# Context feed-forward of a hybrid trunk: half weights in the latents' norm tiles, one norm step to a pair of features, and the decays' chain called from the middle of the loop

## The chip, the cores and the metric

One core of one Trainium2 chip. The metric is the device time of one execution in microseconds (us), as the median of several runs. The engines are named as in the profile: PE (TensorE matmuls), DVE (VectorE), ACT (ScalarE), POOL (GpSimd) and SP (SyncE, which here only issues transfers).

## The reference

One layer (DEPTH is 1) of a diffusion backbone over 1024 latent tokens and 256 context tokens, width 1024, feed-forward width 2816, all in float32. Cut to what the change touches:

```python
x = x + 0.5 * m_l[2] * swiglu(modulate(rms_norm(x, norm1_w), m_l[0], m_l[1]), w1, w3, w2)
ctx = ctx + 0.5 * m_c[2] * swiglu(modulate(rms_norm(ctx, norm1_w), m_c[0], m_c[1]), w1, w3, w2)
y_l, _ = token_mixing(modulate(rms_norm(x, norm2_w), m_l[3], m_l[4]),     # latents
                      modulate(rms_norm(ctx, norm2_w), m_c[3], m_c[4]), ...)
x = x + m_l[5] * y_l
x = x + 0.5 * m_l[8] * swiglu(modulate(rms_norm(x, norm3_w), m_l[6], m_l[7]), v1, v3, v2)
return rms_norm(x, final_norm_w)

def swiglu(h, w1, w3, w2):
    return (silu(h @ w1) * (h @ w3)) @ w2
# in token_mixing, for the retention heads:
lg_f, lg_b = log_sigmoid(ret_decay_f), log_sigmoid(ret_decay_b)
```

## The kernel before

**Arithmetic.** A float32 matrix product is made of three products of a faster type: each operand is split into a hi part (a copy to fp32r, ACT, line 60) and a lo part (the rest, line 61, on DVE or, where `eng` says so, on POOL), and `mm3` (lines 65 to 67) adds hi·hi, lo·hi and hi·lo in PSUM. A tile pair `hh`/`hl` holds the two parts of an activation, `whi`/`wlo` those of a streamed weight; `raw` is the weight as it comes from memory. There are six `raw` buffers and six pairs of `whi`/`wlo`.

**Stages.** `run` goes through the opening of the latents' first feed-forward (0 to some 120 us), its body (to some 650 us), the context's feed-forward (some 645 to 845 us), the latents' last part and the context's projections, the token mixing from about 930 us on, and the second feed-forward. Activations lie transposed: features on the 128 partitions, tokens along a row. `x[0]` and `x[1]` are the two halves of the latents with eight tiles of 128 x 512 each (`KD` is 8), `x[2]` the context with eight tiles of 128 x 256.

**The context's feed-forward.** A feature `f` is 128 of the 2816 hidden columns; the loop takes them in eleven pairs, numbered 0 to 10 below. `classic` (a pair) loads four weights (w1 and w3 of two features), each as two halves of 128 x 512, so eight half weights. Half weight `2 * (i % 4) + j` is split into slot `h00` to `h07` of the pool `hp`, from the second feature on (`halves_slots`, line 274); its lo part is made on POOL (`CENG`). A slot can be written only when PE has read what the pair before left there. One weight gives one `psa` product of 24 matmuls. In the middle of the pair `Y` adds the pair before to the context: eight units of six matmuls each into `psb`, of which there are four banks, each added to `x` by DVE (line 600). `Y` streams its own weights through `raw`, `whi` (ACT) and `wlo` (DVE).

**The norm beside it.** After each pair one entry of `pend` is called: `norm2(1, i)`, the steps of the second norm of the latents' second half: squares, the column of reciprocal roots (`nr`, with a `pow` on POOL), its rows (`ndiag` on DVE, `nrb` on ACT), and for each of eight tiles `norm_k`: `nt` (DVE, line 217, two buffers), `hh` (ACT, line 218), `hl` (DVE, line 223). All eight pairs of tiles `h[1]` are allocated ahead of the loop by `alloc_h((1,), self.hp)`.

**The order.** Most of the program's order is made by a scheduler: each instruction goes into its engine's queue by its priority and by what it depends on, and the queue runs in that order. So the place of a call in the code is not the place of its instructions. The opening's order on PE, DVE and ACT is fixed by hand.

**The decays.** `lg_setup` (line 840) loads eight numbers, spread over 128 partitions, and computes their log-sigmoid by a `pow` on POOL and a series on DVE, all on tiles of 128 x 8; then four small tables `kd` and the factor `cdec` by an exponential on ACT. `mix_setup` calls it at the start of the mixing.

Of the kernel before, what the change touches and what calls it, by code (L numbers as in the profile page):

```python
# [19 lines left out]
KD = D // P  # L20
# [11 lines left out]
class Trunk:  # L32
# [241 lines left out]
    def halves_slots(self, i):  # L274
        if i < 2:
            return None, None
        return tuple(self.hslot(f"0{2 * (i % 4) + j}") for j in range(2))

    def load_halves(self, src, dst=(None, None), eng=None):
        return [self.load_half(src[:, 512 * i:512 * i + 512], dst[i], eng) for i in range(2)]  # L280
# [212 lines left out]
    def back6(self, keep=True):  # L493
        A = self.bank4(self.psA)
        self.prod(1, A, True)
        c1 = self.keep4(A)
        B = self.bank4(self.psB)
        self.prod(2, B, True)
        self.add4(0, 0, self.plus4(c1, B))
        self.prod(6, A, False)  # L500
        u2 = self.keep4(A)
        B = self.bank4(self.psB)
        self.prod(5, B, True)
        c5 = self.keep4(B)
        self.prod(7, A, False)
        if keep:
            u3 = self.keep4(A)
            self.add4(1, 1, self.plus4(c5, u3))
        else:
            self.add4(1, 1, self.plus4(c5, A))  # L510
            self.add4(0, 1, A)
        self.prod(3, B, False)
        self.add4(1, 0, self.plus4(u2, B))
        return A
# [322 lines left out]
            act(a, a, AF.Exp, scale=-1.0)  # L837
            act(a, a, AF.Ln, bias=1.0)

    def lg_setup(self):  # L840
        nc, I, cp = self.nc, self.I, self.cp2
        x = self.tile(cp, [P, 8], F32, "lgx")
        nc.sync.dma_start(x, I["decay"].broadcast_to([P, 8]))
        e = self.tile(cp, [P, 8], F32, "lge")
        nc.vector.memset(e, float(np.e))
        u = self.tile(cp, [P, 8], F32, "lgu")
        nc.vector.tensor_scalar(out=u, in0=x, scalar1=-1.0, scalar2=None, op0=ALU.mult)
        nc.vector.tensor_tensor(out=u, in0=u, in1=x, op=ALU.min)
        nc.gpsimd.tensor_tensor(out=u, in0=e, in1=u, op=ALU.pow)
        t = self.tile(cp, [P, 8], F32, "lgt")  # L850
        nc.vector.tensor_scalar(out=t, in0=u, scalar1=2.0, scalar2=None, op0=ALU.add)
        nc.vector.reciprocal(t, t)
        nc.vector.tensor_tensor(out=u, in0=u, in1=t, op=ALU.mult)
        nc.vector.tensor_tensor(out=t, in0=u, in1=u, op=ALU.mult)
        nc.vector.tensor_scalar(out=e, in0=t, scalar1=1.0 / 19, scalar2=1.0 / 17, op0=ALU.mult, op1=ALU.add)
        for m in (15, 13, 11, 9, 7, 5, 3, 1):
            nc.vector.tensor_tensor(out=e, in0=e, in1=t, op=ALU.mult)
            nc.vector.tensor_scalar(out=e, in0=e, scalar1=1.0 / m, scalar2=None, op0=ALU.add)
        nc.vector.tensor_tensor(out=e, in0=e, in1=u, op=ALU.mult)
        nc.vector.tensor_scalar(out=x, in0=x, scalar1=0.0, scalar2=None, op0=ALU.min)  # L860
        nc.vector.scalar_tensor_tensor(out=x, in0=e, scalar=-2.0, in1=x, op0=ALU.mult, op1=ALU.add)
        self.lg = x
        self.kd = {}
        for i, (nm, s, pos) in enumerate((("f", 0, 2), ("f0", 0, 3), ("b", 4, 0), ("b1", 4, 1))):
            t = self.tile(cp, [P, 4], F32, "kd" + nm)
            nc.vector.tensor_scalar(out=t, in0=x[:, s:s + 4], scalar1=self.tab[:, POSC + pos:POSC + pos + 1],
                                    scalar2=None, op0=ALU.mult)
            nc.scalar.activation(t, t, AF.Exp)
            self.kd[nm] = t
        self.cdec = self.tile(cp, [P, 8], F32, "cdec")  # L870
        nc.scalar.activation(self.cdec, x, AF.Exp, scale=float(P))
# [572 lines left out]
    def run(self):  # L1444
        nc, tc, I = self.nc, self.tc, self.I
# [70 lines left out]
        def norm_step(tg, i, a, b):  # L1516
            with self.low(NLOW if tg == 1 and i in (1, 2) else None):
                norm_part(tg, i, a, b)
# [16 lines left out]
        norm2 = lambda tg, i: norm_step(tg, i, self.mcol(4, int(tg == 2)), self.mcol(3, int(tg == 2)))  # L1535
# [31 lines left out]
        def spill(tg):  # L1567
            o = TGS[tg][0]
            for k in range(KD):
                nc.sync.dma_start(self.xd[k * P:(k + 1) * P, o:o + 512], self.x[tg][k])  # L1570

        self.alloc_h((1,), self.hp)
        norm2(1, 0)
        pend = [lambda i=i: norm2(1, i) for i in range(1, 3 + KD)] + [lambda: spill(1)]
        for f in range(0, NF, 2):
            self.classic(f, (2,), mid2=(lambda: self.Y(f - 2, CT)) if f else None, eng=[nc.gpsimd if e else None for e in CENG])
            pend.pop(0)()
        A = self.bank4(self.psA)
        self.prod(4, A, True)
        self.add4(0, 1, A)  # L1580
# [184 lines left out]
```

## Time and profile before

| What | Value |
|---|---|
| median of 3 runs | 2179.47 us (2178.03 to 2180.61) |
| the profiled execution | 2180.54 us, span 2178.8 us, mean granted clock of PE 0.99 |
| PE busy | 2121.3 us, 97% of the span |
| DVE busy | 1525.0 us, 70% |
| ACT busy | 980.7 us, 45% |
| POOL busy | 280.4 us, 13% |
| traffic | 373 MB, 171 GB/s mean |

All spans of instructions and waits below are of the one profiled execution. A row of the timeline reads: start in us, duration in us, engine, line, operation, output <- inputs, and in brackets the idle time of the engine ahead of it and what ended it. In a row by stretches (`A:B`) follow the length, the busy time of PE, PEld (weight loads into PE), DVE, ACT and POOL with the number of instructions, then the granted clock of PE (1.00 is full), the share of DMA and GB/s.

### The profile page before, as it was taken

How to read it: one execution, taken by the hardware profiler on the slowest of the kernel's cores; microseconds unless marked ns; L12 is line 12 of the kernel's file. 1: busy time of each engine (PE TensorE's matmuls, PEld its weight loads, DVE VectorE, ACT ScalarE, POOL GpSimd, SP SyncE). 2: the span in 40 equal slices, each digit the busy share in tenths (PEclk: the TensorE clock that was granted, in tenths of full speed). 3: DMA queues.
4: the chain of work that ended last, by engine and by line, in shares of the span. 5: the costliest groups of instructions: out<-in, count | busy, mean ns of one | idle time of the engine just before them, and what ended most of it. 6: DMA issues, size and time to landing. Idle time of an engine off the chain costs nothing. (4 is left out here: it accounts for less than half of the span.)

```text
span 2178.8 us, 32819 instructions
## 1 busy us (share of the span) xinstructions
PE 2121.3 (97%) x11558; PEld 1811.5 (83%) x11558; DVE 1525.0 (70%) x2735; ACT 980.7 (45%) x1811; POOL 280.4 (13%) x285
## 2 busy tenths in 40 slices
PE   8999999999999999999989999999999999999998
PEld 7888888888889999987778988788878888888888
DVE  7889999756766756834665546758777666675676
ACT  4433334345545444546454335425343433444553
POOL 0000000000026562611132113200000000010000
PEclk8999999999999999999999999999999999999999
DMA  9267768469966565553322312324134444467674
GB/s 331 83 231 239 267 221 268 167 221 325 306 210 193 156 183 171 180 152 100 92 65 63 98 57 88 122 83 162 63 120 161 146 160 159 150 217 251 207 241 147
DMA packets 202933, 373.39 MB, mean 171 GB/s; under 512 B 24016, under 2 KB 37264, under 8 KB 202768
## 3 DMA queue, kind: packets, MB, share of 16 engines
q1 hardware_dynamic: 202336, 371.16, 52.7%
q8 instruction: 90, 1.47, 0.3%
q14 instruction: 75, 0.61, 0.1%
q10 hardware_dynamic: 432, 0.13, 0.0%
HBM read 296.72 MB, written 66.09 MB: 167 GB/s over the span
## 5 line engine op out<-in xcount | busy, mean ns | idle before, releaser
L60 ACT ACTIVATE whi<-raw 128x512 fp32r<-128x512 f32 (+1 forms) x563 | 347.1, 622 | 621.1 <-PE psa L66 169.1
L61 DVE TENSOR_TENSOR wlo<-raw,whi 128x512 fp32r<-128x512 f32 (+1 forms) x533 | 368.1, 694 | 314.3 <-ACT whi L60 310.9
L65 PE MATMUL psa<-hh,whi 128*128 128x512 f32 (+1 forms) x1108 | 435.2, 393 | 0.1
L66 PE MATMUL psa<-hl,whi 128*128 128x512 f32 (+1 forms) x1108 | 434.6, 392 | 0.0
L67 PE MATMUL psa<-hh,wlo 128*128 128x512 f32 (+1 forms) x1108 | 434.3, 392 | 0.0
L65 PE MATMUL psb<-hh,whi 128*128 128x512 f32 (+1 forms) x680 | 260.0, 382 | 0.5 <-ACT whi L60 0.5
L67 PE MATMUL psb<-hh,wlo 128*128 128x512 f32 (+1 forms) x680 | 259.7, 382 | 0.6 <-DVE wlo L61 0.6
L66 PE MATMUL psb<-hl,whi 128*128 128x512 f32 (+1 forms) x680 | 259.7, 382 | 0.0
L65 PEld LDWEIGHTS psa<-hh,whi 128*128 128x128 f32 x1108 | 209.1, 189 | 42.1 <-ACT s L341 0.6
L67 PEld LDWEIGHTS psa<-hh,wlo 128*128 128x128 f32 x1108 | 209.0, 189 | 41.7
L66 PEld LDWEIGHTS psa<-hl,whi 128*128 128x128 f32 x1108 | 209.1, 189 | 41.3
L65 PEld LDWEIGHTS psb<-hh,whi 128*128 128x128 f32 x680 | 127.9, 188 | 25.9 <-ACT whi L60 1.0
L67 PEld LDWEIGHTS psb<-hh,wlo 128*128 128x128 f32 x680 | 127.8, 188 | 25.7 <-DVE wlo L61 1.0
L66 PEld LDWEIGHTS psb<-hl,whi 128*128 128x128 f32 x680 | 127.9, 188 | 24.8
L60 ACT ACTIVATE hh<-raw 128x512 fp32r<-128x512 f32 x180 | 110.4, 623 | 72.7 <-PE psa L66 44.3
L61 POOL TENSOR_TENSOR hl<-raw,hh 128x512 fp32r<-128x512 f32 x84 | 116.2, 1393 | 70.5 <-ACT hh L60 64.4
L1095 POOL TENSOR_TENSOR nr<-nr,mhalf 128x4 f32<-128x4 f32 (+1 forms) x11 | 10.6, 964 | 869.3 <-DVE nr L1094 869.3
L65 PE MATMUL psa<-hh,hh 128*128 128x256 f32 x376 | 107.8, 287 | 0.0
L67 PE MATMUL psa<-hh,hl 128*128 128x256 f32 x376 | 107.8, 287 | 0.0
L66 PE MATMUL psa<-hl,hh 128*128 128x256 f32 x376 | 107.8, 287 | 0.0
L66 PE MATMUL psa<-wlo,hh 128*128 128x256 f32 (+1 forms) x320 | 93.8, 293 | 1.6 <-DVE wlo L61 1.5
L65 PE MATMUL psa<-whi,hh 128*128 128x256 f32 (+1 forms) x320 | 93.5, 292 | 1.2 <-ACT s L1049 1.2
(402 smaller groups left out, 4251.7 us busy)
## 6 DMA issues: line engine op xcount, KB each, us to landing
raw<-in_w SPq DMA_DIRECT2D x374, 256.0 KB, 3.2
gd<-s SPq DMA_DIRECT2D x154, 256.0 KB, 2.8
ada<-in_adaT SPq DMA_DIRECT2D x76, 512.0 KB, 4.8
raw<-gd SPq DMA_DIRECT2D x91, 256.0 KB, 3.0
s<-in_w SPq DMA_DIRECT2D x66, 256.0 KB, 5.0
sd<-s SPq DMA_DIRECT2D x44, 256.0 KB, 2.9
raw<-sd SPq DMA_DIRECT2D x44, 256.0 KB, 3.1
hh<-in_w SPq DMA_DIRECT2D x44, 256.0 KB, 3.9
```

Source lines behind the costliest of these rows:

```text
L60: nc.scalar.activation(hi, src, AF.Copy)
L61: (eng or nc.vector).tensor_tensor(out=lo, in0=src, in1=hi.bitcast(F32), op=ALU.subtract)
L65: mm(ps, wa[0], xa[0], start=start, stop=False, skip_group_check=more)
L66: mm(ps, wa[0], xa[1], start=False, stop=False, skip_group_check=more)
L67: mm(ps, wa[1], xa[0], start=False, stop=stop, skip_group_check=more)
L1095: nc.gpsimd.tensor_tensor(out=r, in0=r, in1=self.mhalf[:, :n], op=ALU.pow)
```

## The change

Three edits. The last half weight (`i % 4 == 3`, `j == 1`) of the pairs 2 to 9 goes to slot `1{p-2}`, that is to the tiles that will hold `h[1][p-2]`, where it went to slot `07`. The tiles of `h[1]` are no longer allocated ahead of the loop: after pair 2 + k, `norm1(k)` takes slot `1{k}` for `h[1][k]` and calls that tile's norm. And `lg_setup` is cut in two: the load and the chain become `lg_start`, called in the loop at `f == 8` with its tiles in the pool `cp`; the tables `kd` and `cdec` stay in `lg_setup`.

```diff
@@ -274,7 +274,8 @@
     def halves_slots(self, i):
         if i < 2:
             return None, None
-        return tuple(self.hslot(f"0{2 * (i % 4) + j}") for j in range(2))
+        p, last = i // 4, i % 4 == 3
+        return tuple(self.hslot(f"1{p - 2}" if last and j and 2 <= p < 10 else f"0{2 * (i % 4) + j}") for j in range(2))
@@ -837,8 +838,8 @@
-    def lg_setup(self):
-        nc, I, cp = self.nc, self.I, self.cp2
+    def lg_start(self):
+        nc, I, cp = self.nc, self.I, self.cp
         x = self.tile(cp, [P, 8], F32, "lgx")
         nc.sync.dma_start(x, I["decay"].broadcast_to([P, 8]))
...
@@ -860,6 +861,9 @@
         self.lg = x
+
+    def lg_setup(self):
+        nc, cp, x = self.nc, self.cp2, self.lg
         self.kd = {}
@@ -1569,12 +1573,19 @@
-        self.alloc_h((1,), self.hp)
+        self.h[1] = []
         norm2(1, 0)
-        pend = [lambda i=i: norm2(1, i) for i in range(1, 3 + KD)] + [lambda: spill(1)]
+
+        def norm1(k):
+            self.h[1].append(self.hslot(f"1{k}"))
+            norm2(1, 3 + k)
+
+        pend = [lambda i=i: norm2(1, i) for i in (1, 2)] + [lambda k=k: norm1(k) for k in range(KD)] + [lambda: spill(1)]
         for f in range(0, NF, 2):
             self.classic(f, (2,), mid2=(lambda: self.Y(f - 2, CT)) if f else None, eng=[nc.gpsimd if e else None for e in CENG])
             pend.pop(0)()
+            if f == 8:
+                self.lg_start()
```

On PE no instruction changes its place. Three places on other engines follow; lines from 278 on are numbered one higher in the changed kernel, from 866 on four higher.

**DVE in the opening** (some 57 to 64 us). Before, the last tile's `x` is followed by the sum of two weights into `ada` and by the tile's `hl`:

```order
L217 SCALAR_TENSOR_TENSOR x_17_106<-x_17_106,modl_88,nrb_272 128x512
L714 TENSOR_TENSOR ada_139_573<-raw_578,ada_138_572 128x512
L714 TENSOR_TENSOR ada_139_573<-raw_582,ada_138_572 128x512
L223 SCALAR_TENSOR_TENSOR hl_33_133<-x_17_106,modl_88,hh_32_132 128x512
L178 TENSOR_TENSOR nacc_515<-nacc_515,nsq_605 128x512
```

In the changed kernel:

```order
L217 SCALAR_TENSOR_TENSOR x_17_106<-x_17_106,modl_88,nrb_272 128x512
L848 TENSOR_SCALAR lgu_7193<-lgx_7189 128x8
L849 TENSOR_TENSOR lgu_7193<-lgu_7193,lgx_7189 128x8
L861 TENSOR_SCALAR lgx_7189<-lgx_7189 128x8
L852 TENSOR_SCALAR lgt_7197<-lgu_7193 128x8
L853 RECIPROCAL lgt_7197<-lgt_7197 128x8
L854 TENSOR_TENSOR lgu_7193<-lgu_7193,lgt_7197 128x8
L855 TENSOR_TENSOR lgt_7197<-lgu_7193 128x8
L856 TENSOR_SCALAR lge_7191<-lgt_7197 128x8
L715 TENSOR_TENSOR ada_139_573<-raw_578,ada_138_572 128x512
L715 TENSOR_TENSOR ada_139_573<-raw_582,ada_138_572 128x512
L223 SCALAR_TENSOR_TENSOR hl_33_133<-x_17_106,modl_88,hh_32_132 128x512
```

Eight steps of the chain have moved in, of which the fourth (`lgt` at line 852) waits for POOL's `pow`; the rest of the chain follows between the later instructions of the opening. On POOL the `pow` stands between two `nr` of the opening, on SP the load stands behind the first weights' loads.

**ACT in pair 2** (some 675 to 685 us). Here the names carry their slot: `hh06` and `hh07` are the last weight's two halves, `whi` the weights of `Y`. Before:

```order
L581 ACTIVATE s_1422_6378<-psa_1421_6353 128x256
L60 ACTIVATE hh06_1483_6645<-raw_1487_6649 128x512
L60 ACTIVATE whi_1466_6564<-raw_1465_6562 128x512
L60 ACTIVATE whi_1469_6570<-raw_1468_6568 128x512
L60 ACTIVATE hh07_1485_6647<-raw_1488_6653 128x512
L60 ACTIVATE ghi_1430_6418<-s_1422_6378 128x256
```

In the changed kernel:

```order
L582 ACTIVATE s_1406_6362<-psa_1405_6337 128x256
L60 ACTIVATE hh10_1469_6631<-raw_1472_6637 128x512
L60 ACTIVATE hh06_1467_6629<-raw_1471_6633 128x512
L60 ACTIVATE whi_1450_6548<-raw_1449_6546 128x512
L60 ACTIVATE whi_1453_6554<-raw_1452_6552 128x512
L60 ACTIVATE whi_1497_6760<-raw_1496_6758 128x512
L60 ACTIVATE ghi_1414_6402<-s_1406_6362 128x256
```

The last half, now in slot `10`, has moved from behind the two weights of `Y` to ahead of them and of its own first half.

**DVE in pair 3** (some 703 to 715 us). `nt` and `hl` are the norm, `x_946` the addition that frees the first bank of `Y`. Before:

```order
L217 SCALAR_TENSOR_TENSOR nt_6687<-x_832_4111,modl_88,nrb_6435 128x512
L61 TENSOR_TENSOR glo_6684<-s_6643,ghi_6683 128x256
L61 TENSOR_TENSOR wlo_7029<-raw_7026,whi_7028 128x512
L217 SCALAR_TENSOR_TENSOR nt_6941<-x_833_4112,modl_88,nrb_6435 128x512
L223 SCALAR_TENSOR_TENSOR hl_1323_5975<-nt_6687,modl_88,hh_1322_5974 128x512
L217 SCALAR_TENSOR_TENSOR nt_7195<-x_834_4113,modl_88,nrb_6435 128x512
L61 TENSOR_TENSOR wlo_7035<-raw_7032,whi_7034 128x512
L223 SCALAR_TENSOR_TENSOR hl_1325_5977<-nt_6941,modl_88,hh_1324_5976 128x512
L587 TENSOR_TENSOR s_6728<-psa_6742,s_6728 128x256
L223 SCALAR_TENSOR_TENSOR hl_1327_5979<-nt_7195,modl_88,hh_1326_5978 128x512
L61 TENSOR_TENSOR glo_6769<-s_6728,ghi_6768 128x256
L600 SCALAR_TENSOR_TENSOR x_946_4498<-psb_6784,modc_89,x_946_4498 128x256
```

In the changed kernel:

```order
L61 TENSOR_TENSOR wlo_7017<-raw_7014,whi_7016 128x512
L217 SCALAR_TENSOR_TENSOR nt_6673<-x_832_4111,modl_88,nrb_6419 128x512
L61 TENSOR_TENSOR glo_6668<-s_6627,ghi_6667 128x256
L61 TENSOR_TENSOR wlo_7023<-raw_7020,whi_7022 128x512
L217 SCALAR_TENSOR_TENSOR nt_6929<-x_833_4112,modl_88,nrb_6419 128x512
L223 SCALAR_TENSOR_TENSOR hl_1477_6672<-nt_6673,modl_88,hh_1476_6671 128x512
L217 SCALAR_TENSOR_TENSOR nt_7185<-x_834_4113,modl_88,nrb_6419 128x512
L588 TENSOR_TENSOR s_6714<-psa_6728,s_6714 128x256
L601 SCALAR_TENSOR_TENSOR x_946_4498<-psb_6770,modc_89,x_946_4498 128x256
```

Two of the three `hl` and one `glo` have left the place ahead of `x_946`. In each of the later pairs there stands one `hl` and one `nt`, where the pair after this one held the rest of the eight before and the others held none.

## The prediction

> **What bounds the kernel now.** I read the page first: how busy each engine is, then the chain that ended last.
>
> ```profile
> PE 2121.3 (97%) x11558; PEld 1811.5 (83%) x11558; DVE 1525.0 (70%) x2735; ACT 980.7 (45%) x1811; POOL 280.4 (13%) x285
> ```
>
> TensorE works 97% of the span, so a change that leaves the matmuls alone can only move PE's gaps: the profiled execution took 2180.54 us (span 2178.8), of which 57.5 us are not matmul time. The next view is what PE waits for around the edit (waits of PE, 620 to 900 us: engine, line, releaser: us in total, times, longest).
>
> ```profile
> PE psb L65 <- DVE x L600: 7.3, 4, 3.7
> ```
>
> All of it is one kind of wait: the units of `Y` use four PSUM banks in turn, and a fifth unit starts only when DVE has added the first to `x` (line 600). The timeline of PE has the three large ones, and one of the opening (start, duration, what; in brackets the gap before it and who ended it); the fourth of `Y` is what is left of the 7.3, 0.7 us.
>
> ```profile
> 57.23 0.50 PE L66 MATMUL psa<-hl,wh 128*128 128x512 f32 x1 [1.58 <-DVE hl L223]
> 679.17 0.39 PE L65 MATMUL psb<-ghi,whi 128*128 128x256 f32 x1 [1.88 <-DVE x L600]
> 715.15 0.58 PE L65 MATMUL psb<-ghi,whi 128*128 128x256 f32 x1 [3.67 <-DVE x L600]
> 736.15 0.39 PE L65 MATMUL psb<-ghi,whi 128*128 128x256 f32 x1 [0.99 <-DVE x L600]
> ```
>
> A gap costs more than its length. Busy time by stretches, with the granted clock after POOL's column:
>
> ```profile
> 57.50:60.00 2.50, 2.50 (x12) 2.04 (x12) 1.18 (x3) 2.12 (x4) 0.00 (x0) 1.00 0.66 213
> 677.50:680.00 2.50, 0.83 (x6) 0.83 (x7) 2.04 (x3) 0.95 (x2) 2.36 (x2) 0.97 0.59 173
> 680.00:682.50 2.50, 2.50 (x14) 2.50 (x13) 1.74 (x5) 0.00 (x0) 0.24 (x1) 0.50 0.68 211
> 715.00:717.50 2.50, 2.35 (x11) 2.35 (x12) 2.33 (x6) 0.72 (x1) 0.00 (x0) 0.50 0.26 93
> 717.50:720.00 2.50, 2.50 (x13) 2.50 (x13) 1.88 (x4) 0.00 (x0) 0.00 (x0) 0.50 0.00 0
> 720.00:722.50 2.50, 2.50 (x19) 2.50 (x19) 2.02 (x5) 0.33 (x1) 0.00 (x0) 0.84 0.65 210
> ```
>
> After the gap of 3.67 the clock is 0.50 from 715.15 to about 720.8 (0.84 in the last row: a third of it at half speed), so some 5.65 us at half speed, 2.8 us lost; the gap of 1.88 starts such a stretch too, and the one of 1.58 at the opening starts none.
>
> **Part 1: norm steps one to a pair.** Why PE waited 3.67 us stands in DVE's queue of that pair:
>
> ```profile
> 703.73 1.42 DVE L217 SCALAR_TENSOR_TENSOR nt<-x,modl,nrb 128x512 f32<-128x512 f32 x1 [0.65 <-ACT nrb L1530]
> 706.01 1.78 DVE L217 SCALAR_TENSOR_TENSOR nt<-x,modl,nrb 128x512 f32<-128x512 f32 x1
> 707.71 1.78 DVE L223 SCALAR_TENSOR_TENSOR hl<-nt,modl,hh 128x512 fp32r<-128x512 f32 x1
> 709.53 1.67 DVE L217 SCALAR_TENSOR_TENSOR nt<-x,modl,nrb 128x512 f32<-128x512 f32 x1
> 711.73 0.74 DVE L223 SCALAR_TENSOR_TENSOR hl<-nt,modl,hh 128x512 fp32r<-128x512 f32 x1
> 712.72 1.64 DVE L223 SCALAR_TENSOR_TENSOR hl<-nt,modl,hh 128x512 fp32r<-128x512 f32 x1
> 714.62 0.87 DVE L600 SCALAR_TENSOR_TENSOR x<-psb,modc,x 128x256 f32<-128x256 f32 x2
> ```
>
> Three `nt` and three `hl` stand ahead of the addition at 714.62 that frees the bank. The changed order keeps three `nt` there and one `hl`, puts the addition ahead of `glo`, and feeds the weights' lo parts earlier (their raw buffers come free a step sooner, since a last half weight no longer waits for a slot). Replayed with these rows: nt 704.0 to 705.4, glo and a weight's lo to 706.4, nt to 708.1, hl to 709.8, nt to 711.5, `s` to 711.8, addition to 712.3. PE could start its fifth unit at 715.15 - 3.67 = 711.48, so about 0.9 us of the gap stays (0.3 to 1.9), 2.8 go, and a gap of that length leaves the clock alone (even the 1.58 at 57.23 did). Term: -2.8 - 2.8 = **-5.6** (-6.5 to -1.8; at the weak end the gap is still 1.9 us and the clock still drops). The next pair's burst of norm steps goes as well, and with it the gap at 736.15: **-1.1** with a 0.1 us gap beside it (to 0).
>
> What is paid: every later pair now holds one `nt` and one `hl`. A pair without norms today:
>
> ```profile
> 749.51 0.69 DVE L61 TENSOR_TENSOR wlo<-raw,whi 128x512 fp32r<-128x512 f32 x1 [1.84 <-ACT whi L60]
> 750.81 1.11 DVE L61 TENSOR_TENSOR wlo<-raw,whi 128x512 fp32r<-128x512 f32 x1 [0.62 <-ACT whi L60]
> 752.18 0.47 DVE L600 SCALAR_TENSOR_TENSOR x<-psb,modc,x 128x256 f32<-128x256 f32 x1
> 753.88 0.28 PE L65 MATMUL psb<-ghi,whi 128*128 128x256 f32 x1
> ```
>
> The addition ends at 752.65 and the fifth unit starts at 753.88: 1.2 us of slack, with 1.84 + 0.62 us of idle DVE ahead of it. The two steps cost 2 x 0.74 to 2 x 1.78 us. They just fit: **+0.3** for seven pairs (0 to 2).
>
> **Part 2: the last half weight's new slot.** In before the fourth weight's second half has to wait on ACT until PE is through with its slot, and stands behind the two weights of `Y`; now it waits for its transfer alone and stands ahead of them. Where the first gap falls:
>
> ```profile
> 674.86 0.33 SPq L261 DMA_DIRECT2D raw<-in_w  x1
> raw<-in_w SPq DMA_DIRECT2D x8, 256.0 KB, 3.0
> 676.78 0.63 ACT L60 ACTIVATE hh<-raw 128x512 fp32r<-128x512 f32 x1 [0.30 <-DMA raw<-in_w]
> 677.32 1.13 ACT L60 ACTIVATE whi<-raw 128x512 fp32r<-128x512 f32 x2
> 682.92 0.63 ACT L60 ACTIVATE hh<-raw 128x512 fp32r<-128x512 f32 x1 [4.47 <-PE psa L66]
> 677.96 0.76 DVE L61 TENSOR_TENSOR wlo<-raw,whi 128x512 fp32r<-128x512 f32 x1 [2.31 <-ACT whi L60]
> ```
>
> (SP's queue, then the transfers of 670 to 680: median us to land.) DVE's lo part waits for `whi`, with the addition for the bank behind it. The load issued at 674.86 is the last half's; 3.0 us under way it lands near 677.9, and two `hh` of 0.54 us each then stand before `whi`: 679.0 against 677.32, so the gap grows by 1.7 us to 3.6. Of these the stretch at half speed, which starts anyway, gives back some 0.5 us, being shorter by 1 us of work. Term: **+1.2** (0, if the transfer lands sooner, to +3.5 with a longer slow stretch). In the next pair the same order is hidden: there `whi` waits for PE, not for the transfer, and from then on ACT is ahead of its loads' use.
>
> **Part 3: the decays' chain.** The call stands at the fifth pair, but the operations depend on nothing there, and the order puts them at the program's beginning: on SP behind the first weights' loads, on DVE ahead of `ada` and of one `hl` that PE awaits, with POOL's `pow` in between. Where they stand now they cost this:
>
> ```profile
> 932.42 0.17 DVE L847 TENSOR_SCALAR lgu<-lgx 128x8 f32<-128x8 f32 x1 [3.08 <-DMA lgx<-in_decay]
> 932.87 1.78 POOL L849 TENSOR_TENSOR lgu<-lge,lgu 128x8 f32<-128x8 f32 x1 [5.42 <-DMA crv<-s]
> 934.69 0.93 DVE L851 TENSOR_SCALAR lgt<-lgu 128x8 f32<-128x8 f32 x1 [1.53 <-POOL lgu L849]
> 937.41 0.40 PE L66 MATMUL psa<-wlo,hh 128*128 128x288 f32 x1 [1.18 <-DVE wlo L61]
> 941.03 0.21 ACT L871 ACTIVATE cdec<-lgx 128x8 f32<-128x8 f32 x1 [7.63 <-DVE lgx L861]
> 946.77 0.28 PE L945 MATMUL psb<-ident,p 128*32 128x128 f32 x1 [0.91 <-ACT p L944]
> ```
>
> PE's 1.18 comes from a `wlo` queued behind the chain, its 0.91 from ACT, whose weights stood behind `cdec` for 7.63 us. Both go: **-2.0** (-2.4 to 0; a table load of ACT that moves earlier could take it back).
>
> At the opening:
>
> ```profile
> 57.10 0.74 DVE L217 SCALAR_TENSOR_TENSOR x<-x,modl,nrb 128x512 f32<-128x512 f32 x1
> 59.16 1.29 DVE L714 TENSOR_TENSOR ada<-raw,ada 128x512 fp32r<-128x512 f32 x2 [1.32 <-ACT ada L710]
> 60.37 0.75 DVE L223 SCALAR_TENSOR_TENSOR hl<-x,modl,hh 128x512 fp32r<-128x512 f32 x1
> 61.45 0.39 PE L66 MATMUL psa<-hl,wh 128*128 128x512 f32 x1
> ```
>
> DVE is free at 57.84. From the chain's first step to the one behind `pow` are 934.69 - 932.42 = 2.27 us, then come five steps of some 0.2 (0.17 in `lgu`'s row): `ada` starts near 61.1 where it started at 59.16, its wait of 1.32 being used up. The `hl` ends near 63.1, and PE needs it at 61.45: a new gap of **+1.7** (0.9, were `pow` done in half its time; 2.9, if the steps behind it are as long as `lgt`'s 0.93). The waits of PE list nothing more up to 640 us that could take it back. SP's one more issue, of 4 KB, is taken as hidden by the lead of the loads (3.0 us to land, above).
>
> **Sum:** -5.6 - 1.1 + 0.3 + 1.2 - 2.0 + 1.7 = -5.5: the profiled execution would be 2175.0. It lay 1.07 above the median of the runs, 2179.47; from that, **2174.0**.
>
> **The rivals.** Under 0.2% (4.4 us) a measurement of this kernel cannot be told from no change; so faster means under 2175.1, slower over 2183.8. For two of them, what POOL does beside the burst of norm steps:
>
> ```profile
> 705.38 3.56 POOL L61 TENSOR_TENSOR hl<-raw,hh 128x512 fp32r<-128x512 f32 x2 [0.78 <-ACT hh L60]
> ```
>
> Rival 1, the burst's gap stays long. DVE's `nt` and `hl` take 0.74 alone and 1.64 to 1.78 beside POOL's splits, and three `nt` are still there. With a gap of 1.9 left, the clock drops as after 679.17, and the part brings 1.8 in place of 5.6: -1.7, **2177.8**. For it: my replay ends only 0.9 us above free. The Trainium skill (TensorE: Matmul & The Clock Gate, Part 1) has the half rate only after an idle window of about 3.4 us; by it a gap of 1.9 would keep the clock and this rival would give -4.5. The rows at 677.5 and 680 differ: 1.88 us was enough.
>
> Rival 2, the new gap at the opening also drops the clock: 1.7 us lies between the 1.58 at 57.23, after which the trace shows no drop, and the 1.88 that had one. Half speed for 5.65 us costs 2.8 more, a late `pow` 1.2: -1.5, **2178.0**. It decides from a gap of some 1.6 to 1.9 us on.
>
> Rival 3, slower: in each of seven pairs `nt` and `hl` meet POOL's splits, as those of 706 to 711 did, and the addition comes later than its 1.2 us of slack. At 3.56 us for the two against 2.46 of idle and 1.2 of slack they fit by 0.1; if POOL's splits in turn hold up the raw buffers and the lo parts, an overshoot of 1.9 us a pair gives +13.3 for +0.3: +7.5, **2187.0**. It is slower than the bound from an overshoot of 1.5 us on. Against it: the lo parts also get their transfers earlier. The Trainium skill (SBUF — State Buffer, Who interferes with whom) says that a DVE instruction with two SBUF inputs contends with a GpSimd instruction that reads SBUF and that the loser blocks for the whole instruction. The 1.78 against 0.74 agree with it, and by it spreading the norm over all pairs meets more splits, not fewer.
>
> Rival 4, more is won: the last half's transfer lands with the others (part 2 costs 0), `pow` is short (0.9), and the terms reach their good ends, -6.5 - 1.1 - 2.4: -9.1, **2170.4**.
>
> **How the numbers follow.** Forecast 0.43 (its own range 2171 to 2177, three quarters of it under 2175.1), rival 1 0.16, rival 2 0.13, rival 3 0.18, rival 4 0.10. Faster: 0.32 + 0.10 = 0.42; same: 0.11 + 0.16 + 0.13 = 0.40; slower 0.18. For 8 in 10 the range takes in all but rival 3: 2169 below, with a little under rival 4, and 2182 above, where rivals 1 and 2 with the +2 of the pairs end.
>
> **What would show it.** In the changed trace: a gap of PE near 61.5 of 1 to 3 us, released by DVE's `hl`; a gap of 3 to 4 us near 681; about 1 us near 714 with the clock at 1.00 after it; none near 736; steady pairs without a gap; and near 937 no wait for `wlo`. I am wrong if the gap near 714 stays over 1.9, if the later pairs show gaps released by line 601, or if the clock halves near 62.

## The result and the profile after

The changed kernel takes 2195.39 us (median of 6 runs, 2187.01 to 2197.94), the kernel before 2180.04 (6 runs, 2178.03 to 2181.19): ratio 1.0065, 95% interval 1.0046 to 1.0084. The profiled execution took 2197.59 us, its span 2195.8. It is slower by about 15 us where 5.5 us were to be gained.

The first row of the page of the changed kernel, with busy time, share and count of each engine:

```profile
PE 2129.9 (97%) x11558; PEld 1810.7 (82%) x11558; DVE 1528.1 (70%) x2735; ACT 978.1 (45%) x1811; POOL 279.3 (13%) x285
```

PE does the same 11558 instructions and is busy 8.6 us longer (2121.3 before): part of the loss is no waiting at all. The waits of PE by line, in total, times and longest (620 to 900, 900 to 990 and 50 to 130 us):

```profile
PE psb L65 <- DVE x L601: 11.4, 8, 3.5
PE psa L65 <- ACT s L1053: 4.3, 2, 3.0
PE psa L66 <- DVE hl L223: 2.8, 2, 1.6
```

The first row was 7.3 us in four waits; now there are eight. Of PE's timeline here are the forecast gap of the opening, the two that answer to 679.17 and 715.15 of before, and three that were not forecast:

```profile
63.96 0.50 PE L66 MATMUL psa<-hl,wh 128*128 128x512 f32 x1 [1.24 <-DVE hl L223]
685.39 0.58 PE L65 MATMUL psb<-ghi,whi 128*128 128x256 f32 x1 [3.52 <-DVE x L601]
718.23 0.38 PE L65 MATMUL psb<-ghi,whi 128*128 128x256 f32 x1 [0.76 <-DVE x L601]
754.66 0.39 PE L65 MATMUL psb<-ghi,whi 128*128 128x256 f32 x1 [1.62 <-DVE x L601]
811.61 0.39 PE L65 MATMUL psb<-ghi,whi 128*128 128x256 f32 x1 [2.19 <-DVE x L601]
943.26 0.40 PE L65 MATMUL psa<-whi,hh 128*128 128x288 f32 x1 [3.00 <-ACT s L1053]
```

The gap of 3.67 us has shrunk to 0.76 and the one at 736 is gone, as forecast. But of the five later `Y` up to 845 us, which had no gap, four have one: besides the two shown 0.70 us at 791.70 and 1.25 at 831.30. What that is worth shows in the view by stretches, whose number behind PE counts its matmuls. Of the kernel before:

```profile
740.00:820.00 80.00, 80.00 (x670) 80.00 (x668) 37.94 (x69) 39.55 (x75) 50.57 (x38) 1.00 0.60 182
150.00:450.00 300.00, 300.00 (x1310) 244.98 (x1309) 277.56 (x459) 115.34 (x203) 0.00 (x0) 1.00 0.69 226
1600.00:1900.00 300.00, 300.00 (x1323) 247.80 (x1322) 203.08 (x332) 119.29 (x208) 0.00 (x0) 1.00 0.47 155
```

Of the changed kernel, with three stretches that begin behind a gap ahead of them:

```profile
64.00:66.50 2.50, 2.50 (x11) 2.08 (x12) 2.43 (x7) 1.79 (x4) 0.00 (x0) 1.00 0.52 195
754.70:757.20 2.50, 2.40 (x13) 2.19 (x14) 2.50 (x6) 1.00 (x2) 1.73 (x2) 0.74 0.88 270
811.60:814.10 2.50, 2.39 (x17) 2.18 (x18) 2.45 (x6) 1.06 (x3) 1.79 (x2) 1.00 0.82 251
740.00:820.00 80.00, 75.20 (x609) 73.95 (x609) 47.16 (x72) 37.38 (x73) 46.58 (x34) 0.98 0.50 160
150.00:450.00 300.00, 300.00 (x1306) 244.31 (x1305) 279.02 (x461) 114.62 (x202) 0.00 (x0) 1.00 0.69 228
1600.00:1900.00 300.00, 300.00 (x1305) 244.34 (x1304) 203.86 (x332) 118.13 (x207) 0.00 (x0) 1.00 0.46 152
```

From 740 to 820 us PE does 61 matmuls fewer (80 / 670 = 0.119 us each): 7.3 us. From 1600 to 1900 us, in the second feed-forward, it does 18 fewer (0.2268 us each) though it is busy all the time at full clock: 4.1 us in 300, and 4.8 from 1500 to 1985 us by the starts of the same matmuls in both traces. The change has no operation in that stage.

### The profile page after: what moved, and what is told of

Its sections match the earlier page's. It is cut to its first block, busy times and chain, and to the rows that moved or that the text cites. A ratio compares the mean times of both kernels' runs of the same rounds, so it can differ in the third digit from the quotient of the medians.

```text
span 2195.8 us, 32829 instructions
## 1 busy us (share of the span) xinstructions
PE 2129.9 (97%) x11558; PEld 1810.7 (82%) x11558; DVE 1528.1 (70%) x2735; ACT 978.1 (45%) x1811; POOL 279.3 (13%) x285
```

## The experiments

Ratios are to runs of the kernel before on the same chip, with their 95% intervals; 0.001 is 2.2 us. The runs come from several chips, so two of them are compared by their ratios; a ratio goes by all runs and can differ by some 2 us from that of the medians. The column "matmuls" of the table is the count of 740 to 820 us in each profile (670 before).

| Run | Median us | Ratio | Matmuls |
|---|---|---|---|
| e1 address alone | 2185.06 | 1.0030 (1.0017 to 1.0042) | 676 |
| e2 change, address put right | 2188.29 | 1.0043 (1.0027 to 1.0059) | 624 |
| e7 first feed-forward put right | 2177.81 | 0.9996 (0.9988 to 1.0004) | 669 |
| e3 parts 1 and 2 | 2185.47 | 1.0033 (1.0021 to 1.0045) | 622 |
| e4 part 3, address right | 2184.53 | 1.0020 (1.0011 to 1.0028) | 669 |
| e9 part 3 late | 2179.49 | 1.0002 (0.9990 to 1.0014) | 669 |
| e5 first half in place of last | 2189.76 | 1.0041 (1.0026 to 1.0055) | 626 |
| e6 parts 1 and 2, no norm steps | 2181.42 | 1.0014 (1.0003 to 1.0025) | 636 |
| e12 nt ahead | 2182.29 | 1.0018 (1.0007 to 1.0028) | 633 |
| e13 slots one pair later | 2180.64 | 1.0002 (0.9988 to 1.0015) | 615 |
| e14 e13 and address | 2180.17 | 1.0001 (0.9990 to 1.0012) | 627 |
| e15 before, no norm steps | 2174.32 | 0.9967 (0.9957 to 0.9978) | 669 |
| e16 own raw buffer | 2182.78 | 1.0016 (1.0007 to 1.0026) | 669 |
| e17 norm in DVE's idle time | 2183.34 | 1.0022 (1.0012 to 1.0032) | 597 |
| e18 norm earlier | 2180.08 | 1.0008 (0.9997 to 1.0020) | 606 |
| e19 e17 and address | 2179.30 | 1.0006 (0.9997 to 1.0015) | 595 |
| e21 load order on ACT | 2172.52 | 0.9974 (0.9964 to 0.9984) | 669 |
| e23 e21 and address | 2170.34 | 0.9963 (0.9948 to 0.9977) | 669 |

### The slow matmuls: an address

The chain's four tiles of 128 x 8 take 32 bytes a partition each. Moved from `cp2` to `cp` they shift every pool that is allocated from the left of SBUF, the memory of the tiles, by 128 bytes, the streamed weights among them (`whi` from 81024 to 81152), while the tiles allocated from the right, such as `t1h` at 163712, stay. Three rows of PE's timeline of the changed kernel, six matmuls apart:

```profile
1661.35 0.39 PE L65 MATMUL psa<-hh,whi 128*128 128x512 f32 x1
1662.71 0.40 PE L65 MATMUL psa<-t1h,whi 128*128 128x512 f32 x1
1664.10 0.40 PE L65 MATMUL psa<-t1h,whi 128*128 128x512 f32 x1
```

Six matmuls take 1.36 us where `hh` moves (allocated from the left like the weights) and 1.39 where `t1h` and `t1l` do. Over 1550 to 1985 us, worked out from the starts of the matmuls and the allocation (steps over 0.25 us, which are gaps, left out): 0.2273 us a matmul (1110 of them) where the moving tile and the weights have the same address modulo 256, 0.2328 (762) where not; in the kernel before all 1897 had the same, at 0.2268. In the first feed-forward the kernel before has 314 at 0.2335, whose addresses are 96 and 128 modulo 256. Three runs test it (theory A).

> The kernel before with one change: 128 bytes of padding behind the constants, so that every tile of the left pools (activations hh/hl, raw, whi, wlo) lies 128 bytes higher, as it does in the changed kernel; no other instruction but one small memset on POOL. Theory A (addresses): a matmul of 512 columns is slower by 3% when its moving tile and its weights differ in their address modulo 256. Then the 514 matmuls of the second feed-forward that ran at 0.2328 in the changed kernel do so here, the first feed-forward loses 1 us more, and the time is 5 to 8 us above before (2185 to 2188), with no gap of PE changed. Rival B: the slow matmuls were a state of that execution, or came from the changed order. Then the pitch is 0.227 throughout the second feed-forward and the time is that of before within 2 us.

```diff
         self.mod = [self.tile(cp, [P, 72], F32, "modl"), ...]
+        self.pad(cp, 32)
```

One padding of 128 bytes in the kernel before, and nothing else, costs 5.5 us (2185.06 against 2179.56). The view by stretches of this run:

```profile
1600.00:1900.00 300.00, 300.00 (x1306) 244.63 (x1306) 200.06 (x326) 117.24 (x205) 0.00 (x0) 1.00 0.46 150
```

> The changed kernel with 128 bytes of padding behind the constants, so that its left pools lie 256 bytes higher than before instead of 128; the order of the instructions is the changed kernel's. Theory A (addresses modulo 256): the second feed-forward runs at a pitch of 0.227, the first as before, and the time is 5 to 7 us below the changed kernel's 2195.4, so 2188 to 2191, while the gaps of the opening, of the later pairs and near 943 stay. Rival B (the order makes the matmuls slow): 2194 to 2197.

The same padding in the changed kernel (128 + 128 bytes) brings the count back. The ratio falls from 1.0065 to 1.0043, some 5 us, though the two intervals overlap:

```profile
1600.00:1900.00 300.00, 300.00 (x1323) 247.86 (x1322) 203.68 (x332) 120.34 (x209) 0.00 (x0) 1.00 0.47 153
```

> The kernel before with 224 bytes of padding in the right pool dp, so that the first feed-forward's tiles in xp (96 modulo 256 before, while the weights are at 128) come to 128 modulo 256. No other edit. Theory A: the 314 matmuls of 130 to 480 us that ran at 0.2335 run at 0.227, and those behind them that caught up: 2 to 3.5 us less than before, 2176.5 to 2178. Rival B: no change.

```diff
         self.dp = opn("dp", "right")
+        self.pad(self.dp, 56)
```

In the kernel before, the padding puts the first feed-forward's tiles at the weights' address modulo 256: 1316 matmuls from 150 to 450 us where there were 1310, and all at 0.2270. In the time its 2 us do not stand out of the noise (0.9988 to 1.0004). So the address effect is shown in the matmuls by all three runs, and in the time by e1: it follows the difference modulo 256, not the address, and nothing but padding was changed. What makes it inside the chip no run shows.

### The parts by themselves

> Parts 1 and 2 of the change alone: the last half weight in the norm's tiles, one norm step to a pair; the decays' chain and all addresses as before. If the later pairs' gaps (754, 791, 811, 831 in the changed kernel) come from these parts, the loop over the context loses 3 to 4 us against before by its end (gain of some 7 near 715 and 736, loss of 2 near 680 and of 8 in the later pairs), the opening and the stretch from 930 on are as before, and the second feed-forward runs at a pitch of 0.227: 2182 to 2186. If they came from the moved chain or the addresses, the loop gains 5 us and the time is 2174 to 2176.

Parts 1 and 2 alone (the diff without `lg_start`, so that no address moves) cost 1.0033, and the count of 740 to 820 us is 622: the later pairs' loss comes from here.

> Part 3 of the change alone (the decays' chain as its own function, called in the loop at f == 8, tiles in cp), and 128 bytes of padding more, so that the left pools lie 256 bytes higher than before. Theory A: at 256 bytes the pitch of the second feed-forward is 0.227 again. The opening shows the gap near 61.5 (with what stands before it, +2.5 us against before), the loop over the context is as before, and near 940 PE waits for the copies of line 1053 instead of the chain (0 to +2.5): 2182 to 2185. Rival B, or the chain being harmless: within 2 us of before.

Part 3 alone, with the padding of e1, so that the left pools move by 256 bytes: 1.0020. The later pairs are whole (669). The opening has the forecast gap:

```profile
62.68 0.50 PE L66 MATMUL psa<-hl,wh 128*128 128x512 f32 x1 [1.21 <-DVE hl L224]
```

and from 900 to 990 us PE waits 3.5 us for ACT and 4.5 in all (in the kernel before 4.3 in all): nothing is gained.

> Part 3 alone, with the chain's working tiles in a pool that is opened only at the end of the first feed-forward, so that the chain runs near 650 us instead of in the opening; left pools 256 bytes higher than before. If the chain's cost lay in the opening (1.4 us) and in what took its place near 940 (0 to 2 us), the opening is as before here, PE shows no new gap near 650, and the stretch from 930 on is that of the run with part 3 alone: 2179 to 2183. If the longer time of that run came from elsewhere, it stays at 2184 to 2185.

```diff
-        nc, I, cp = self.nc, self.I, self.cp
+        nc, I, cp = self.nc, self.I, self.sp       # the pool n2
...
+        self.lg = self.tile(self.cp, [P, 8], F32, "lg")
```

With the working tiles in the pool `n2`, and the left pools again 256 bytes higher, the chain cannot run at the opening. It runs not near 650 us, as expected, but from 456 us (its load) to 476, where PE shows no gap either; there is no gap near 62, and the time is that of the kernel before. So part 3's place in the opening costs some 4 us by the ratios (1.0020 against 1.0002, with intervals that overlap), of which the trace shows a gap of 1.2. The two profiled executions are themselves only 1.2 us apart (2182.57 and 2181.41 us), so a rest is not in these traces, and whether there is one stays open.

### The later pairs: four theories

The norm's `nt` stands between the two late `wlo` of `Y` on DVE, beside POOL's splits (theory N, the prediction's third rival). Or ACT's queue is at fault (theory H). In the changed kernel, on ACT, DVE and SP around 800 us:

```profile
798.34 1.68 ACT L60 ACTIVATE hh<-raw 128x512 fp32r<-128x512 f32 x3 [5.60 <-DMA raw<-in_w]
806.08 0.63 ACT L60 ACTIVATE whi<-raw 128x512 fp32r<-128x512 f32 x1 [4.21 <-DMA raw<-in_w]
806.74 0.69 DVE L61 TENSOR_TENSOR wlo<-raw,whi 128x512 fp32r<-128x512 f32 x1 [1.93 <-ACT whi L60]
807.35 1.80 DVE L217 SCALAR_TENSOR_TENSOR nt<-x,modl,nrb 128x512 f32<-128x512 f32 x1
809.07 1.76 DVE L61 TENSOR_TENSOR wlo<-raw,whi 128x512 fp32r<-128x512 f32 x1
811.09 0.47 DVE L601 SCALAR_TENSOR_TENSOR x<-psb,modc,x 128x256 f32<-128x256 f32 x1
800.36 0.33 SPq L261 DMA_DIRECT2D raw<-in_w  x1
```

The program's order of these four `hh` on ACT, by the numbers of their tiles, is not that of their loads on SP:

```
SP   raw_8163 raw_8167 raw_8202 raw_8206      (issued 790.95 791.37 792.08 793.51, landed 793.54 794.78 795.42 798.32)
ACT  hh_1815<-raw_8206  hh_1805<-raw_8163  hh_1807<-raw_8167  s  hh_1813<-raw_8202
```

`hh_1815` is the half weight with the new slot. It has no matmul to wait for, so the scheduler puts it first; its transfer lands last. ACT waits 5.60 us for it with three landed halves behind it, POOL cannot split these, their raw buffers stay taken, and SP issues no load between 794.14 and 800.36: by the allocation the load at 800.36 goes to the buffer of `raw_8206` itself, and so waits for POOL's split of that newest half. The raw tile of `Y`'s weight lands at 806.05, `whi` starts at 806.08. From 737 to 837 us ACT waits like this six times. What its `hh` waited for there, in total, times and longest, first in the kernel before, then in the changed one:

```profile
ACT hh L60 <- PE psa L66: 32.7, 22, 3.6
ACT hh L60 <- DMA raw<-in_w: 25.0, 6, 5.6
```

> Parts 1 and 2 as in the run with them alone, but the norm's tiles take the first half weight of a pair (i % 4 == 0, j == 0) instead of the last: its transfer is the first of the pair's eight, so ACT does not wait for the youngest transfer with older loads behind it, and the last half goes back to slot 07 behind the weights of Y. One norm step a pair as before. Theory H (the later pairs' gaps come from ACT waiting for the last half's transfer ahead of loads that have landed): the gaps of the later pairs vanish and the one near 680 goes back to 1.9, the loop gains 5 to 8 us against before: 2172 to 2175. Theory N (they come from nt and hl beside POOL's splits): the later pairs still lose 1 us each: 2180 to 2185.

```diff
-        p, last = i // 4, i % 4 == 3
+        p, first = i // 4, i % 4 == 0      # and: if first and not j
```

626 matmuls, 1.0041. I first took this as the end of H. It is not: the profile has the same pattern,

```profile
799.98 1.67 ACT L60 ACTIVATE hh<-raw 128x512 fp32r<-128x512 f32 x3 [5.52 <-DMA raw<-in_w]
```

since the scheduler puts the half of the next pair (`raw_8217`) ahead of four halves that were loaded before it. The edit did not take away what it was to take away.

> Parts 1 and 2 alone, with the last half in the norm's tiles as in the change, but each of the eight norm steps of the latents' second half is left out and replaced by two copies of x on ACT, so that nt and hl are off DVE in this loop (the second half's norm is not computed, and the result is not the reference's). Theory H: the gaps of the later pairs stay at more than half of their 6 to 7 us: 2179 to 2183. Theory N: they vanish, while 680 keeps its longer gap and 715 and 736 are gone: 2172 to 2175.

The norm's steps are left out (two copies of `x` on ACT fill each `h[1]`). The time falls to 1.0014, and I read that as theory N. But the count, 636, stays far from 670: without a single `nt` or `hl` on DVE most of the later pairs' loss is still there.

> Parts 1 and 2 alone, as in the run with the slots and the norm, but each of the eight norm calls raised in priority, so that from the second tile on nt stands ahead of both late wlo of Y on DVE and no longer between them. Theory Q (the place in DVE's queue): DVE is idle 1.83 us ahead of the first of these wlo (at 801.42 in that run) and POOL's splits start only at 801.99, so nt takes some 0.74 us there and costs nothing; the gaps of PE after 720 us, which were 1.41, 0.93 and 0.78, fall under 0.4 each, the gap of 3.6 near 683 stays, and the ratio falls from 1.0033 to about 1.001 (2182 us against 2179.5). Theory P (sharing with POOL costs the same wherever nt stands): gaps of 0.7 us or more remain in three or more of the later pairs and the ratio stays near 1.003.

```diff
-            norm2(1, 3 + k)
+            with self.tc.high_priority(offset=400):
+                norm2(1, 3 + k)
```

`nt` stands ahead of both `wlo` and takes 0.74 us, but `glo` beside POOL's splits is long, and gaps are kept (633 matmuls; the ratio lies between the two that were expected). DVE's timeline:

```profile
800.71 0.74 DVE L217 SCALAR_TENSOR_TENSOR nt<-x,modl,nrb 128x512 f32<-128x512 f32 x1
806.01 1.51 DVE L61 TENSOR_TENSOR glo<-s,ghi 128x256 fp32r<-128x256 f32 x1 [0.43 <-ACT ghi L60]
```

> As the run before with nt ahead, and the last half weight changes its slot one pair later (pairs 3 to 10 in place of 2 to 9, each norm call one pair later). If the gap of 3.6 us near 683 comes from the two hh that stand ahead of Y's whi while the last half's transfer is under way, it goes back to the 1.9 us of the kernel before, and the pair after hides the same order, since its whi waits for PE; the burst of three nt stays broken up, so that no gap over 1.5 us stands at 715 or 736. Then PE waits 3 us or less in all from 640 to 900 us and the ratio is about 0.998 (2175 to 2177 us). If the order of pair 2 only moves to the next pair, a gap over 3 us with the clock at half speed stands near 700 and the ratio is 1.0 to 1.002.

As e12, but the slots change in pairs 3 to 10 (`3 <= p < 11`, `p - 3`). As expected, the gap of 3.5 us near 684 goes back to 1.55, which belongs to the order in pair 2; the later pairs lose as before (615), and the ratio is 1.0002, not 0.998. With the padding of e7 it is no better:

> As the run with the slots one pair later, and 224 bytes of padding ahead of the tiles xp of the first feed-forward, which puts them at the same address modulo 256 as its weights. If both effects add, the matmuls of 150 to 450 us number 1316 where before had 1310, some 2 us are gained over that run, and the ratio is 0.997 to 0.998 (2173 to 2175 us), which would be faster than the kernel before. If the address effect brings nothing in the time, the ratio is that of the run it is built on.

So neither the norm's presence nor its place is the cause. Two causes remained: the new slot itself, or the lead that the loads win while PE stands still at 715 us.

> The kernel before with its own slots; only the nt and hl of the latents' second half are left out (two copies of x on ACT fill each h[1] in their place). The burst of three nt and three hl is gone, and with it PE's gaps at 715 and 736 us (7.5 us with the slow clock). The pairs of features from 754 to 840 us take 17.28 us each in the kernel before, and 17.6 to 20.3 in every run with the new slots, whether the norm's steps lie beside them or not. Theory D (the loads' pace): those 17.28 rest on the lead that the loads of the weights win while PE stands still at 715 and 736; without the stall ACT's hh wait for transfers, the pairs take 17.9 to 18.5 us, some 5 of the 7 us are handed back by 840 us, and the ratio is 0.999 to 1.0005. Theory S (the new slot itself, which puts the last half's hh ahead of Y's whi): with the old slots the pairs stay at 17.28 us, the gain is kept, and the ratio is about 0.997 (2173 us).

The kernel before with its own slots and the norm's steps left out as in e6: 669 matmuls, 0.9967. PE does not need the stall, so the loads' lead is not what was lost (theory D falls); without the norm's steps some 7 us are won by the ratio (4.8 by the medians), near the 6.7 that the prediction had for the burst; and the cost in the later pairs is the new slot's (theory S): e6 differs from this run by the slots alone and has 636.

> The run with nt ahead and the slots one pair later, and the raw tile of the last half weight has a buffer of its own, a seventh beside the six (made room for by one buffer of nrb in place of two). Theory D, with the turn of the six raw buffers as what sets the loads' pace: the loads win a lead, the pairs of 744 to 820 us, 17.9 to 20.3 us in that run, come down to 17.3 to 17.6, the gain at 735 us (-9 in that trace) is kept, and the ratio is 0.997 to 0.998. Theory S: the order on ACT is as in that run and so are the pairs; ratio 1.000 to 1.001.

669 matmuls, but 1.0016, more than either theory had. The order shows why: with a free slot and a buffer of its own every last half is loaded and split by 681 us, at the stage's beginning, where PE now waits, and is missing from the later pairs. It shows that the pairs are whole without that half, not that a buffer was short.

> The kernel before with its own slots and one number changed: the two steps of the latents' norm ahead of the tiles (the column of reciprocal roots and its rows) get a lower priority, so that the first four nt and three hl stand on DVE behind the eight additions of one Y, where DVE was idle some 5 us in the kernel before, and the other norm steps in the next pair, ahead of its wlo and behind its additions. Theory S: with the old slots the pairs without norm stay at 17.28 us, and the burst no longer stands ahead of an addition; PE's 3.67 us with the slow clock after it and the 0.99 at 736 go, and one gap of 1 to 2 us comes in the pair with the rest of the norm. Ratio 0.997 to 0.998 (2173 to 2175 us). Rival: the later place of the norm meets POOL's splits with more of its steps, the gap only moves by one pair and keeps over 1.9 us and the slow clock: ratio 0.9995 to 1.0005.

> As the run before with the priority between: two nt and two hl behind the additions, then two nt, two hl and a third nt ahead of the next pair's first addition, the rest behind it. If what counts is how many norm steps stand ahead of an addition (five here, six in the kernel before), a gap of 1.5 to 3 us is left, with the slow clock if it is over 1.6, and the ratio is 0.998 to 0.9995.

> The first of these three and 224 bytes of padding ahead of xp, which aligned the first feed-forward's tiles with its weights modulo 256. If both add, 150 to 450 us hold 1316 matmuls where the kernel before had 1310, some 2 us more are won, and the ratio is 0.996 to 0.997 (2171 to 2173 us).

Three runs with the old slots: only `NLOW`, by which the norm's reciprocal roots and rows are lowered in priority, goes from 150 to 600, to 450, and to 600 with the padding of e7. The rival had the mechanism: the burst only moves, to gaps of 2.55 and 1.88 us near 765 and 771 in e17. All three times lie above what was expected, the rival's too in e17 (1.0022). Neither of the two priorities holds the norm's steps apart; in the runs with the new slots the slots do that.

> The run with nt ahead and the slots one pair later, with one step added for each of its eight last half weights: a copy of one column of the half weight ahead of it on ACT, so that ACT can take the last half only behind that one, in the order of their loads. Without it ACT's queue has the last half's hh first, which waits for a transfer that was issued after those of the three halves behind it (in the run without the norm it waited 4.10 us to 770.77 for the raw issued at 768.02, while raws that had landed from 766.99 on stood behind it, and SP stood 4.4 us for a raw buffer). Theory H (ACT's head of line): the three halves are split when they land, SP gets its raw buffers in time, ACT's hh wait for PE again and not for transfers, the pairs from 762 to 837 us take 17.3 to 17.5 us where that run had 17.9 to 20.3, and the ratio is about 0.997 (2172 to 2174 us against 2179). Theory P (the norm's steps on DVE beside POOL's splits, one to a pair): the pairs stay at 17.8 us or more and the ratio at 1.000.

```diff
-        return [self.load_half(src[:, 512 * i:512 * i + 512], dst[i], eng) for i in range(2)]
+        r = [self.load_half(src[:, :512], dst[0], eng)]
+        if dst[1] is not None and dst[1] is self.far:      # the half with the new slot
+            self.nc.scalar.activation(dst[1][0][:, :1], r[0][0][:, :1], AF.Copy)
+        return r + [self.load_half(src[:, 512:], dst[1], eng)]
```

One column is copied ahead of each such half, so that ACT takes it behind the half loaded before it. ACT's timeline in a later pair:

```profile
766.07 0.63 ACT L60 ACTIVATE hh<-raw 128x512 fp32r<-128x512 f32 x1 [3.57 <-PE psa L66]
767.50 0.63 ACT L60 ACTIVATE hh<-raw 128x512 fp32r<-128x512 f32 x1 [0.81 <-PE psa L66]
768.95 0.63 ACT L60 ACTIVATE hh<-raw 128x512 fp32r<-128x512 f32 x1 [0.54 <-issue]
769.61 0.20 ACT L285 ACTIVATE hh<-hh 128x1 fp32r<-128x1 f32 x1
769.84 0.63 ACT L60 ACTIVATE hh<-raw 128x512 fp32r<-128x512 f32 x1
774.03 0.64 ACT L60 ACTIVATE whi<-raw 128x512 fp32r<-128x512 f32 x1 [1.57 <-DMA raw<-in_w]
```

These `hh` wait for PE again, no longer for the transfer; by stretches:

```profile
740.00:820.00 80.00, 80.00 (x669) 80.00 (x668) 52.30 (x88) 42.09 (x84) 49.86 (x36) 1.00 0.61 185
```

Every norm step is there, DVE does more in the stretch than in the changed kernel, and PE has no gap: 0.9974. This run decides between H and N, since it differs from e13 (1.0002) by the copies and the order that they bring; e23 below repeats it with a padding. In both runs `nt` stands ahead of both `wlo` and takes 0.74 us, and `hl` meets a split of POOL in nearly every pair (1.60 us at 771.15). The copies put ACT's splits into the order of the loads and with it change which buffer the next load gets; these two are not separated.

> The run before and 224 bytes of padding ahead of xp, which aligns the first feed-forward's tiles with its weights modulo 256. If both add, 150 to 450 us hold 1316 matmuls or more where the kernel before had 1310, and the ratio is 0.996 (2170 to 2172 us), which would be faster than both kernels. If H falls, it is that of e14, 1.000.

With the padding of e7: 2170.34 us, 0.9963, 1316 matmuls from 150 to 450 us. It beats both kernels; its gain over e21 is within the noise (the intervals overlap).

## Why the prediction was wrong, point by point

| Step | Forecast us | Shown |
|---|---|---|
| burst of norm steps, gaps at 715 and 736 | -5.6, -1.1 | right: 0.76 and none; clock 1.00; 6.6 us won from 690 to 742 |
| gap near 681 | +1.2, to 3.6 us | right: 3.52 (1.88 before), from the order in pair 2 (e13) |
| later pairs | +0.3 | **wrong**: 61 matmuls, 7.3 us by 820 us; 8.7 by 845 |
| chain away from 930 us | -2.0 | wrong: waits of 4.8 us for 4.3; 1.5 us lost |
| chain in the opening | +1.7 | near: gap 1.24, clock 1.00, 1.5 us lost; by the ratios some 4 (e4 against e9) |
| matmul rate | no term | **missing**: 5.5 us (e1) |

Followed by the starts of the same matmuls, the two profiled executions end 17.0 us apart: +1.5 in the opening, +1.6 from there to 640 us, +1.5 at 681, -6.6 at 715 and 736, +8.7 in the later pairs, +1.5 near 930 and +4.8 in the second feed-forward. The other 4.0 us, ahead of 57 us, from 950 to 1500 and behind 1985, lie where other runs stray from the kernel before by as much, and have no cause shown.

The later pairs, whose gaps released by line 601 the prediction had named as a sign of being wrong, failed in part 2, in one sentence: that the order in which the last half stands ahead of `Y`'s weights is hidden from the second pair on, "there `whi` waits for PE, not for the transfer, and from then on ACT is ahead of its loads' use". I had looked at what the half stands ahead of, not at what it waits for. Of the three halves behind it the loads come earlier, so in each pair ACT waited for the newest transfer with older ones landed; ACT's lead was lost, and `whi` waited for its transfer too. The same belief stands in part 1 ("their raw buffers come free a step sooner") and against rival 3: they came free later, and SP stood 6.2 us for one. Rival 3 had the sign and the place, but not the cause, and not the price: it gave the later pairs 13.3 us, and its total of +7.5 is half of what was measured. In e6 most of the loss is there without a norm step, and in e21 `hl` meets POOL's splits and no pair is late. The contention that rival 3 rests on is real: `nt` takes 1.80 us at 807.35 beside POOL, and 0.74 at 800.71 of e12, just behind POOL's last split. The Trainium skill (SBUF — State Buffer, Who interferes with whom) has this contention for a DVE instruction with two SBUF inputs and a GpSimd instruction that reads SBUF. In e21 ACT's lead covers that of `hl`; whether it would cover a long `nt` between the two `wlo` no run shows, for there `nt` stands ahead.

The length from which a gap drops the clock, on which rivals 1 and 2 turn (some 1.6 to 1.9 us), is no fixed length in these traces: 1.62 us dropped it at 754.66, 2.19 at 811.61 did not.

Near 930 us the rows of the chain were read rightly, PE's wait for `wlo` fell from 1.5 to 0.2 us; but the order that the scheduler then made put a `whi`, whose raw tile came late, ahead of the copy `s` (line 1053) that frees PE's bank: 3.00 us and the slow clock (0.59 from 943.20 to 945.70). The sum had a price for what leaves this place and none for what is late next in the changed order.

The address had no place in the sum: four tiles of 4 KB were taken as nothing but their instructions.

## What to carry to other kernels

A tile that no longer waits for a slot does not only come sooner: a list scheduler moves it ahead of older work, so compare the order of the splits with the order of their loads on every queue, and look for an instruction that waits for the newest transfer. When only small tiles move between pools, compare the addresses before and after, and count matmuls per stretch in stages that the change does not touch. An experiment that is to remove a cause has first to be shown in the order to have removed it; e5 had not, and cost a wrong turn.

## What was not expected of the hardware

- A matmul of 512 columns takes some 0.227 us (0.2268 to 0.2279 in the traces before and after) where the SBUF addresses of moving tile and weights are equal modulo 256, and 0.2328 to 0.2345 where they differ: 0.2328 at a difference of 128 and 0.2345 at 96 (both in the changed kernel), 0.2335 at 32 (before). Those of 256 columns change the other way: from 740 to 820 us 0.1188 us in e1, where the two lie 128 apart, and 0.1200 before, where they are equal; that is 676 matmuls for 670.
- The slow clock after an idle time is not set by its length alone: in the changed kernel 1.62 us at 754.66 is followed by 0.74, but 1.60 at 58.35 and 2.19 at 811.61 by 1.00; so is 1.95 at 679.33 in e21. What else decides no run shows.
